# Six blocks of layer 2's modulation vectors move from TensorE products to VectorE, four of them into the scan stage

## The chip, the cores and the metric

The kernel runs on one core of one Trainium2 chip. The metric is the device time of one execution in microseconds. Before the change three runs gave 2504.61, 2489.74 and 2491.8 us, with a median of 2491.8 us.

## The reference

The reference is a two-layer trunk over 256 latent tokens and 256 context tokens, width 2048, batch 1. Each layer takes its shift, scale and gate from a conditioning vector, one for the latent tokens (`c`) and one for the context tokens (`c_ctx`).

```python
def adaln_params(cond, w_mod, b_mod):
    return jnp.split(jax.nn.silu(cond) @ w_mod + b_mod, 3, axis=-1)   # shift, scale, gate: 3 x 2048

def modulate(x, gain, shift, scale):
    return rmsnorm(x, gain) * (1 + scale) + shift

def na_mla_layer(x, ctx, c, c_ctx, ...):       # layer 1
    sh, sc, gt = adaln_params(c, w_mod, b_mod)
    hx = modulate(x, norm, sh[:, None], sc[:, None]) @ w_in     # the same for ctx with c_ctx
    ...                                        # 8 neighbourhood heads, 8 latent (MLA) heads
    y = (jnp.concatenate([merge_heads(o_na), merge_heads(o_mla)], axis=-1) * jax.nn.silu(z)) @ w_out
    x = x + gt[:, None] * y                    # ctx too
```

Layer 2 is a gated DeltaNet. Its input is `modulate(...) @ w_in` of both streams. After a short convolution, 32 value heads are scanned in chunks of 64 tokens in two directions, and the result goes through a gated output projection, `x + gt * y`. In layer 2 only the latent tokens are carried on, so its gate is needed for one of the two conditioning vectors, its shift and scale for both. A final RMSNorm ends the trunk.

## The kernel before

A modulation vector of one layer has 6144 columns, cut into 12 chunks of 512: chunks 0 to 3 are the shift, 4 to 7 the scale, 8 to 11 the gate. The weights of a chunk are 16 tiles of 128 x 512, 4 MB in all. The conditioning is `cond`, with one column for each of the two streams (samples, in the code). There are two ways of making a chunk:

- `adaln` (lines 122 to 159), the product on TensorE. Eight loads `mraw` of 512 KB bring the chunk; 16 matmuls `pmod<-mraw,cond` in four column strips of the array sum it up, VectorE copies the sum (`macc`), four transposes `pmt` bring it to one column per 128 values, and VectorE reduces it into `mod`.
- `adaln_lanes` (lines 161 to 192), on VectorE. For each of the 16 tiles and each sample one instruction on all 128 lanes, `lacc = mraw * cond + lacc` (the first of the 16 is a plain multiplication); at the end eight one-column matmuls `pml` against ones sum over the partitions, and VectorE adds the bias.

Both are generators, which a stage of the kernel advances a little at a time: `unit` (a 2048-row product for 128 output rows, in three passes `whi*hx`, `whi*hxlow`, `wlo*hx`, L90 to L92) advances the generator in `ahead` twice, and the loop over the latent heads once a head. A scheduler then sets each engine's order from the dependences and its own costs. Where a call names `after`, the instructions are held behind that matmul in the order of their engine.

The stages on the profile's clock, with what they make of the modulation vectors:

1. Layer 1's projections and its neighbourhood heads 0 to 6, to about 580 us. Layer 1's gate and layer 2's chunks 0 and 1 are made here on VectorE.
2. The latent ranks, 580 to 691 us: the last neighbourhood head's products, and `craw`, eight 512-wide products of 2048 rows, normalised into `cx`. No modulation work.
3. The latent heads (MLA), from 691 us to 900.9 us, where the last value product `po` ends. Here `ahead = later(mr, ((1, (2, 3, 8), 0),))` (L472) makes chunks 2, 3 and 8 by products, and L495 chunk 9, also by products.
4. The output projection with `gx` as its input, until 1066 us: 16 `unit`s. L512 starts `later(mr, ((1, (4, 5, 6, 7), 1),), last_mm)`, the scale chunks on VectorE.
5. The boundary to layer 2, 1066 to about 1145 us. L521 makes chunks 10 and 11 by products. `rstd_bcast` brings the norm's factor `rb`; `modulate` makes layer 2's input `hx` from it, with ScalarE (L236, L241), VectorE (L235, L238) and GpSimd (L243).
6. Layer 2's projections and its head preparation, to about 1742 us.
7. The scans, from about 1742 us. Here the order on TensorE, VectorE and ScalarE is the order of the code (`manual_schedule`). The loop goes over steps `st`; a step runs one chunk of 64 tokens for a pair of value heads in each of two chains (context, and six steps behind it the latent tokens), and, as filler on TensorE, 24 matmuls of the value projection. A step takes some 9.7 us. Weights are loaded as `raw`, three ahead, and split into `whi` (ScalarE) and `wlo` (VectorE). The chain of a step begins with `pks` (L1033); VectorE makes two `R` (L1037) of it, TensorE goes on with `ptr` (L1045), and at the end `ptr` (L1078) is added to `rf` on VectorE (L1083). Every second step ends with the convolution's taps (0, 4) on VectorE (L585), and every fourth has the output's `re` (L1111) behind them.
8. The output projection of layer 2, the gate, and the final norm.

Of the kernel before, what the change touches and what calls it, by code (L numbers as in the profile page):

```python
# [8 lines left out]
F32 = mybir.dt.float32  # L9
F32R = mybir.dt.float32r  # L10
AF = mybir.ActivationFunctionType
ALU = mybir.AluOpType
# [4 lines left out]
KT = 16  # L17
S = 256
T = 512
# [7 lines left out]
def trunk_kernel(ctx: ExitStack, tc: tile.TileContext, g):  # L27
# [16 lines left out]
    def cst(name, shape, src=None):  # L44
        t = const.tile(shape, F32, name=name, tag=name)
        if src is not None:
            nc.scalar.dma_start(t, src)
        return t
# [14 lines left out]
    ab_bmod, dn_bmod = vecs[:, 56:104], vecs[:, 104:152]  # L63
    o_gain = vecs[:, 152:153]
    mods = [cst(f"mod{l}", [128, 48, 2]) for l in range(2)]
    Am = [cst(f"Am{l}", [128, KT, 2]) for l in range(2)]


# [92 lines left out]
    def adaln_lanes(l, ps, pm, tp, chunks, after=None):  # L161

        wm, bmod, gain = ((g["ab_wm"], ab_bmod, ab_gain), (g["dn_wm"], dn_bmod, dn_gain))[l]
        for ch in chunks:
# [26 lines left out]
                V.tensor_tensor(Am[l][:, f], Am[l][:, f], gain[:, f].unsqueeze(2).broadcast_to([128, 4, 2]), op=ALU.mult)  # L191
            yield

    def steps(it, n=1000):
        for _ in range(n):
            if next(it, it) is it:
                break
# [62 lines left out]
    with tc.tile_pool(name="s0", bufs=2) as tp, tc.tile_pool(name="s0p", bufs=1, space=PSUM) as ps:  # L260
        V.memset(cond, 0.0)
        A.activation(cond[:, :, 0:2], cc, AF.Silu)
        xs = ((xA, g["xT"]), (xB, g["cT"]))
        for j in range(0, KT, 4):
            for x, src in xs:
# [53 lines left out]
    with tc.tile_pool(name="ab", bufs=2, reuse_waits="tile") as tp, \  # L319
# [105 lines left out]
        cr = tc.alloc_tile_pool(name="cr", bufs=1, reuse_waits="tile")  # L425


        craw = cr.tile([128, 8, T], F32, name="craw", tag="craw")
        rbl = []
        rbl2 = tp.tile([128, 2, T], F32, name="rbl", tag="vt", bufs=1)  # L430
# [13 lines left out]
        def roped(p, scale, parts_of):  # L444
            out = tp.tile([128, T], F32, name="rope", tag="rope", bufs=1)
            if scale == 1.0:
                A.copy(out, p)
            else:
                A.mul(out, p, scale)
            pp = ps.tile([128, S], F32, name="pp", tag="tr", bufs=TR)  # L450
            PE.matmul(pp, perm, out[:, :S], start=True, stop=True)
            t = tp.tile([128, S], F32, name="rtmp", tag="mtmp")
            V.tensor_tensor(t, pp, sinT, op=ALU.mult)
            V.tensor_tensor(out[:, :S], out[:, :S], cosT, op=ALU.mult)
            V.tensor_tensor(out[:, :S], out[:, :S], t, op=ALU.add)
            for r, hi, lo in parts_of:
                both(hi, lo, out[r])

        kr = tp.tile([128, 2, T], F32R, name="kr", tag="kr", bufs=1)
        roped(krp, 1.0, [(slice(0, 128), kr[:, 0], kr[:, 1])])  # L460
        na7 = na_head(7)
        cx = parts_tile("cx")
        ch, qr = cx[:, 0], cx[:, 1]
# [5 lines left out]
                V.tensor_tensor(ch[:, 8 + j], craw[:, j], ch[:, j].bitcast(F32), op=ALU.subtract)  # L469
        cr.release()  # L470
        mr = tc.alloc_tile_pool(name="mr2", bufs=2, reuse_waits="tile")
        ahead = later(mr, ((1, (2, 3, 8), 0),))  # L472

        rows = slice(0, 64), slice(64, 128)
        attend(*na7)
# [16 lines left out]
            attend(*o, 8 + h, None, ([qr[:, 2 * h + i] for i in range(2)], [kr[:, i] for i in range(2)]))  # L492

        steps(ahead)
        steps(later(mr, ((1, (9,), 0),), last_mm))  # L495
        pace = 0
        gx = parts_tile("gx")
        gh, gl = gx[:, 0], gx[:, 1]
# [19 lines left out]
            if j % 4 == 3:  # L518
                nc.sync.dma_start(x1d[:, j - 3:j + 1], x1[0][:, j - 3:j + 1])
        steps(ahead)  # L520
        ahead = later(mr, ((1, (10, 11), 0),), last_mm)  # L521
        rb = rstd_bcast(blocks_of(qacc, sq), 4, D, ps, "st", tp)
        hx = parts_tile("hx")
        hh, hl = hx[:, 0], hx[:, 1]
        modulate(1, lambda k, s: x1[s][:, k], rb, hh, hl, tp)
        steps(ahead)
        mr.release()

    abx.release()
# [110 lines left out]
    with tc.tile_pool(name="dn", bufs=2, reuse_waits="tile") as tp, \  # L640
# [288 lines left out]
        room = {}  # L929
# [192 lines left out]
        W += [g["dn_wo"][u][:, 1024 * c:1024 * c + 1024] for u, c in wo_order]  # L1122
        raws, wt = [], []

        def hi():
            j = len(wt)
            if j < len(W):
                while len(raws) < min(len(W), j + 3):
                    raws.append(load_raw(W[len(raws)]))
                h = wp.tile([128, 1024], F32R, name="whi", tag="whi", bufs=3)  # L1130
                A.copy(h, raws[j])  # L1131
                wt.append([h])
# [22 lines left out]
        def nothing():  # L1155
            return iter(())
# [59 lines left out]
        outs = early()  # L1216
        GATES = {56: (0, 4, 8), 57: (12, 16), 58: (20,), 66: (24,)}
        LAG = 6
        fins = nothing()
        for st in range(-2, 64 + LAG):  # L1220
            i, n = st // 4, st % 4
# [66 lines left out]
                take(fins, 1)  # L1288
            if vals and st % 2 == 1:
                prev = cur  # L1290
            for k in GATES.get(st, ()):
                gate(k, 4)
            if st == 68:
# [146 lines left out]
```

## Time and profile before

| | |
|---|---|
| runs | 2504.61, 2489.74, 2491.8 us, median 2491.8 |
| profiled execution | 2493.04 us, its span in the profile 2491.2 us |
| mean granted TensorE clock | 0.992 |
| TensorE matmuls | busy 2428.2 us (97%) |
| VectorE | busy 1762.8 us (71%) |
| ScalarE | busy 1105.6 us (44%) |
| GpSimd | busy 161.1 us (6%) |
| loads of layer 2's modulation weights | 96 of 512 KB |

An engine's share is an average over all eight stages; what an engine does in one of them is read from the windows of that stage. The chain that ended last is the path followed back from the last instruction, each step to what released it; a row of it says which line held the end of the kernel up and for how long. In a group of instructions, "idle before" is the time for which the engine stood idle just ahead of them, with what ended it. L numbers are lines of the kernel.

### The profile page before, as it was taken

What the parts mean: (1) busy time and instruction counts of PE and PEld (TensorE: products, weight loads), DVE (VectorE), ACT (ScalarE), POOL (GpSimd) and SP (SyncE); (2) the same over time, 40 slices, a digit from 0 to 9 for tenths busy, and PEclk for the clock granted to TensorE, in tenths of its full rate; (3) what the DMA queues carried; (4) which work ended last, traced back from release to release, by engine and by line L of the source; (5) the groups of instructions that cost most, each with busy time, mean ns of one, the idle gap of its engine ahead of it and who ended that gap; (6) DMA issues with size and microseconds to landing.
All of it is one profiled execution on the core that took longest, in us unless ns stands there. A gap on an engine that the chain in (4) does not pass through costs nothing.

```text
span 2491.2 us, 42483 instructions
## 1 busy us (share of the span) xinstructions
PE 2428.2 (97%) x16110; PEld 1963.1 (79%) x16110; DVE 1762.8 (71%) x3538; ACT 1105.6 (44%) x2446; POOL 161.1 (6%) x165
## 2 busy tenths in 40 slices
PE   6999999999989999999999999999999999999998
PEld 4557888888858878858998989987777777777787
DVE  4654678883356687856998988885777777777765
ACT  4223332333254432257565655634444544445453
POOL 0000000000000000020011101000000000012000
PEclk9999999999999999999999999999999999999999
DMA  8872645542253366664665666774343333336454
GB/s 252 282 277 87 200 154 172 169 157 84 88 187 110 102 198 204 226 210 136 195 173 158 179 178 180 204 201 108 87 116 103 115 112 98 106 100 184 148 193 141
DMA packets 254940, 397.24 MB, mean 159 GB/s; under 512 B 122257, under 2 KB 163857, under 8 KB 254609
## 3 DMA queue, kind: packets, MB, share of 16 engines
q1 hardware_dynamic: 253584, 393.00, 52.0%
q8 instruction: 127, 2.08, 0.3%
q10 hardware_dynamic: 1152, 1.54, 0.2%
q14 instruction: 77, 0.62, 0.1%
HBM read 356.94 MB, written 35.39 MB: 157 GB/s over the span
## 4 chain that ended last, share of the span: by engine, by line
PE 88%; issue 5%; DMA 3%; DVE 2%; ACT 1%; SPq 0%; POOL 0%; DVEq 0%; POOLq 0%; ACTq 0%
PE mm L90 21%; PE mm L91 20%; PE mm L92 20%; PE pks L1033 3%; PE pmod L141 3%; PE ptr L1045 2%; PE sp L365 2%; PE mm L105 2%; PE po L365 1%; DMA mraw<-dn_wm 1%; PE ptr L1078 1%; PE psu L1064 1%; PE pks L1064 1%; PE pt L398 1%; PE mm L107 1%
## 5 line engine op out<-in xcount | busy, mean ns | idle before, releaser
L90 PE MATMUL mm<-hx,whi 128*128 128x512 f32 (+1 forms) x2304 | 843.7, 366 | 2.3 <-ACT t L664 2.2
L91 PE MATMUL mm<-hx,whi 128*128 128x512 f32 (+1 forms) x2304 | 820.6, 356 | 2.5 <-issue 2.5
L92 PE MATMUL mm<-hx,wlo 128*128 128x512 f32 (+1 forms) x2304 | 819.4, 356 | 0.6 <-DVE wlo L78 0.6
L77 ACT CAST whi<-raw 128x1024 fp32r<-128x1024 f32 (+2 forms) x346 | 338.6, 980 | 701.4 <-PE mm L91 502.3
L78 DVE TENSOR_TENSOR wlo<-raw,whi 128x1024 fp32r<-128x1024 f32 (+2 forms) x346 | 394.3, 1142 | 204.3 <-ACT whi L77 198.2
L90 PEld LDWEIGHTS mm<-hx,whi 128*128 128x128 f32 x2304 | 438.8, 190 | 106.3 <-issue 27.0
L92 PEld LDWEIGHTS mm<-hx,wlo 128*128 128x128 f32 x2304 | 438.6, 190 | 65.1 <-issue 4.2
L91 PEld LDWEIGHTS mm<-hx,whi 128*128 128x128 f32 x2304 | 438.8, 190 | 61.4 <-issue 9.2
L177 DVE SCALAR_TENSOR_TENSOR lacc<-mraw,cond,lacc 128x512 f32<-128x512 f32 x300 | 208.6, 746 | 0.7 <-DMA mraw<-dn_wm 0.7
L585 DVE SCALAR_TENSOR_TENSOR acc<-cin,taps,acc 128x508 f32<-128x508 f32 (+3 forms) x256 | 187.2, 731 | 20.3 <-ACT acc L576 17.2
L105 PE MATMUL mm<-hx,whi 128*128 128x512 f32 x480 | 173.1, 404 | 0.1
L1055 DVE SCALAR_TENSOR_TENSOR vl<-ptr,egm,vh 128x128 fp32r<-128x128 f32 x224 | 64.7, 346 | 95.1 <-ACT rf L1052 37.9
L107 PE MATMUL mm<-hx,wlo 128*128 128x256 f32 x457 | 128.4, 281 | 1.3 <-DVE wlo L1139 1.2
L141 PE MATMUL pmod<-mraw,cond 128*32 128x512 f32 (+2 forms) x640 | 98.4, 508 | 28.1 <-DMA mraw<-ab_wm 18.8
L1139 DVE TENSOR_TENSOR wlo<-raw,whi 128x1024 fp32r<-128x1024 f32 x84 | 102.5, 1221 | 13.5 <-ACT whi L1131 13.4
L105 PEld LDWEIGHTS mm<-hx,whi 128*128 128x128 f32 x480 | 88.9, 188 | 24.5 <-issue 5.0
L816 DVE SCALAR_TENSOR_TENSOR outer<-L,bv,X 128x31 f32<-128x31 f32 (+15 forms) x248 | 99.4, 401 | 6.4 <-POOL X L811 0.5
L90 PE MATMUL mm<-gx,whi 128*128 128x512 f32 x256 | 100.3, 394 | 3.4 <-DVE x1B L515 2.4
L599 ACT ACTIVATE ac<-acc 128x128 f32<-128x128 f32 x160 | 37.4, 300 | 144.2 <-DVE acc L585 144.1
L91 PE MATMUL mm<-gx,whi 128*128 128x512 f32 x256 | 100.4, 392 | 0.5 <-DVE gx L503 0.5
L92 PE MATMUL mm<-gx,wlo 128*128 128x512 f32 x256 | 99.8, 391 | 0.0
L1049 ACT ACTIVATE vh<-ptr,egm 128x128 fp32r<-128x128 f32 x224 | 71.3, 374 | 57.1 <-PE ptr L1045 55.2
(301 smaller groups left out, 3648.5 us busy)
## 6 DMA issues: line engine op xcount, KB each, us to landing
raw<-dn_w SPq DMA_DIRECT2D x194, 512.0 KB
mraw<-dn_wm SPq DMA_DIRECT2D x96, 512.0 KB
mraw<-ab_wm SPq DMA_DIRECT2D x88, 512.0 KB
raw<-ab_w SPq DMA_DIRECT2D x66, 512.0 KB
raw<-dn_wo SPq DMA_DIRECT2D x64, 512.0 KB
raw<-ab_wo SPq DMA_DIRECT2D x32, 512.0 KB
raw<-ab_w SPq DMA_DIRECT2D x32, 256.0 KB
spt<-sp SPq DMA_DIRECT2D x64, 128.0 KB
```

Of the source, the lines that this page charges most:

```text
L77: A.copy(hi[:, :m], raw[:, :m])
L78: V.tensor_tensor(lo[:, :m], raw[:, :m], hi[:, :m].bitcast(F32), op=ALU.subtract)
L90: PE.matmul(ps, wh[:, c], xh[:, k0 + k, sl], start=first and k == 0, stop=False)
L91: PE.matmul(ps, wh[:, c], xl[:, k0 + k, sl], start=False, stop=False)
L92: end = PE.matmul(ps, wl[:, c], xh[:, k0 + k, sl], start=False, stop=last and k == kt - 1)
L105: PE.matmul(p2, wh[:, c], x[:, :, k0 + k], start=start, stop=stop)
L107: PE.matmul(p2[:, 0], wl[:, c], x[:, 0, k0 + k], start=False, stop=False)
L141: PE.matmul(pmod[32 * q:32 * q + 32, :m], cond[:, 4 * kg + q, :], raw[c // 1024][:, half + c % 1024:half + c % 1024 + m], start=kg == 0, s ...
L177: V.scalar_tensor_tensor(acc[:, s], raw[:, q], cond[:, k, s:s + 1], acc[:, s], op0=ALU.mult, op1=ALU.add)
L585: V.scalar_tensor_tensor(o3[:, :, i0:i1], p3[:, :, i0 + d:i1 + d], taps[:, ch, t:t + 1], o3[:, :, i0:i1], op0=ALU.mult, op1=ALU.add)
L816: V.scalar_tensor_tensor(o, L[:, rows, k:k + 1].broadcast_to([128, n, m]), bv[:, k:k + 1], X[:, k:k + 1, cols].broadcast_to([128, n, m]), ...
L1139: V.tensor_tensor(w, raws[j], h.bitcast(F32), op=ALU.subtract)
```

## The change

A new generator `lanes` makes a chunk on VectorE for `n` samples. Its loads come from the buffers of the weights (`raw`, four, shared with the products' weights), one load ahead.

```
+    cond1 = cst("cond1", [128, KT, 1])
...
+    def lanes(l, chunks, acc_of, cnd, n, pt_of):
+        wm, bmod = ((g["ab_wm"], ab_bmod), (g["dn_wm"], dn_bmod))[l]
+        tiles = [(ch, t) for ch in chunks for t in range(8)]
+        load = lambda ch, t: load_raw(wm[ch, t // 2][:, t % 2 * 1024:t % 2 * 1024 + 1024])
+        ahead = load(*tiles[0])
+        yield
+        for i, (ch, t) in enumerate(tiles):
+            raw, ahead = ahead, load(*tiles[i + 1]) if i + 1 < len(tiles) else None
+            if t == 0:
+                acc = acc_of(ch)
+            for q in range(2):
+                k = 2 * t + q
+                for e in range(n):
+                    x = raw[:, 512 * q:512 * q + 512]
+                    if k == 0:
+                        V.tensor_scalar(acc[e], x, cnd[:, k, e:e + 1], None, op0=ALU.mult)
+                    else:
+                        V.scalar_tensor_tensor(acc[e], x, cnd[:, k, e:e + 1], acc[e], op0=ALU.mult, op1=ALU.add)
+            yield
+            if t == 7:
+                pt = pt_of(n)
+                for j in range(4):
+                    for e in range(n):
+                        PE.matmul(pt[:, j, e:e + 1], acc[e][:, j * 128:j * 128 + 128], ones[:, 0:1], start=True, stop=True)
+                f = slice(4 * ch, 4 * ch + 4)
+                V.tensor_tensor(mods[l][:, f, :n], pt, bmod[:, f].unsqueeze(2).broadcast_to([128, 4, n]), op=ALU.add)
...
+        A.copy(cond1, cond[:, :, 0:1])
...
+        ahead = lanes(1, (2, 3), lambda ch: [tp.tile([128, T], F32, name="lacc", tag="bias") for _ in range(2)], cond, 2,
+                      lambda n: ps.tile([128, 4, n], F32, name="pml", tag="pm", bufs=1))
         craw = cr.tile([128, 8, T], F32, name="craw", tag="craw")
...
+        steps(ahead)
         na7 = na_head(7)
...
-        ahead = later(mr, ((1, (2, 3, 8), 0),))
+        ahead = iter(())
...
-        steps(later(mr, ((1, (9,), 0),), last_mm))
         pace = 0
...
-        ahead = later(mr, ((1, (10, 11), 0),), last_mm)
         rb = rstd_bcast(blocks_of(qacc, sq), 4, D, ps, "st", tp)
...
         modulate(1, lambda k, s: x1[s][:, k], rb, hh, hl, tp)
-        steps(ahead)
...
+        depth = 3
         def hi():
...
-                while len(raws) < min(len(W), j + 3):
+                while len(raws) < min(len(W), j + depth):
...
+        gates = lanes(1, range(8, 12), lambda ch: [room["e"][:, 3072 + 512 * (ch % 2):3584 + 512 * (ch % 2)]], cond1, 1,
+                      lambda n: ps.tile([128, 4, n], F32, name="pml", tag="tr", bufs=1))
...
+            if st == 3:
+                depth = 2
+            if 4 <= st < 56:
+                depth = 2 if next(gates, 0) is None else 3
```

So chunks 2 and 3 (shift) are made for both samples between the `craw` products, the gate's chunks 8 to 11 for the latent sample alone at the end of 32 scan steps, one load and two instructions a step, summed up in free columns of a scan tile (`re`). While they run, the scans' weights are loaded two ahead and not three.

The calls for the scale chunks are not touched in the code, but the scheduler's order changes around them. The first place is VectorE at the start of the latent heads, just behind the last `cx`. Before, the softmax of the last neighbourhood head follows at once (`mx`, `rc`, `pr`), with `vt`, `PT` (copies from PSUM) and a weight's `wlo`:

```order
L469 TENSOR_TENSOR cx<-craw,cx 128x512 x5
L358 TENSOR_TENSOR vt<-pv,vt 128x512
L394 RECIPROCAL rc<-sm 128x1
L395 TENSOR_SCALAR pr<-pr,rc 128x512
L389 TENSOR_REDUCE mx<-sp 128x1
L394 RECIPROCAL rc<-sm 128x1
L395 TENSOR_SCALAR pr<-pr,rc 128x512
L78 TENSOR_TENSOR wlo<-raw,whi 128x512
L358 TENSOR_TENSOR PT<-pt,PT 128x4x128
```

Now, with line numbers moved by the new code (by 1 to 34 here):

```order
L503 TENSOR_TENSOR cx<-craw,cx 128x512 x5
L176 TENSOR_SCALAR lacc<-mraw,cond 128x512 x2
L389 TENSOR_TENSOR vt<-pv,vt 128x512
L178 SCALAR_TENSOR_TENSOR lacc<-mraw,cond,lacc 128x512 x2
L425 RECIPROCAL rc<-sm 128x1
L178 SCALAR_TENSOR_TENSOR lacc<-mraw,cond,lacc 128x512 x2
L426 TENSOR_SCALAR pr<-pr,rc 128x512
L420 TENSOR_REDUCE mx<-sp 128x1
L425 RECIPROCAL rc<-sm 128x1
L178 SCALAR_TENSOR_TENSOR lacc<-mraw,cond,lacc 128x512 x2
L420 TENSOR_REDUCE mx<-sp 128x1
L79 TENSOR_TENSOR wlo<-raw,whi 128x512
```

The `lacc` rows are the scale chunks 4 to 7. They stood in the output projection before, and now stand between the softmax instructions of the latent heads: all 128 of them come ahead of the split of `gx`. Their loads moved with them on the load queue, to between the latent heads' weights, where the loads of the products stood.

The second place is VectorE at the end of a scan step with `st % 4 == 0`. Before, the taps and `re` are followed by the next step's `R`:

```order
L1083 TENSOR_TENSOR rf<-rf,ptr 128x256
L585 SCALAR_TENSOR_TENSOR acc<-cin,taps,acc 128x2x254 x2
L1111 SCALAR_TENSOR_TENSOR re<-pot,ngain,re 128x512
L1037 SCALAR_TENSOR_TENSOR R<-pks,neg,ra 128x128 x2
L1037 SCALAR_TENSOR_TENSOR R<-pks,neg,vc 128x128 x2
```

Now (the same lines are L1114, L616, L1142 and L1068):

```order
L1114 TENSOR_TENSOR rf<-rf,ptr 128x256
L616 SCALAR_TENSOR_TENSOR acc<-cin,taps,acc 128x2x254 x2
L1142 SCALAR_TENSOR_TENSOR re<-pot,ngain,re 128x512
L214 SCALAR_TENSOR_TENSOR re<-raw,cond_85,re 128x512 x2
L1068 SCALAR_TENSOR_TENSOR R<-pks,neg,ra 128x128 x2
L1068 SCALAR_TENSOR_TENSOR R<-pks,neg,vc 128x128 x2
```

The gate's two instructions of a step (`cond_85` is `cond1`) stand behind everything of the step and ahead of the next step's `R`; at the other steps with gate work they stand in the same place, behind `rf` alone or behind `rf` and the taps.

The third place is TensorE at the boundary to layer 2. Before, the products of chunks 10 and 11 stand between the norm's sums, `rb` and layer 2's first products:

```order
L204 MATMUL ss<-ones,sq 128x1
L141 MATMUL pmod<-mraw,cond 32x512 x6
L213 MATMUL rb<-dg,ones 128x128 x4
L141 MATMUL pmod<-mraw,cond 32x512 x2
L90 MATMUL mm<-hx,whi 128x512 x2
L141 MATMUL pmod<-mraw,cond 32x512 x4
L91 MATMUL mm<-hx,whi 128x512
```

Now:

```order
L234 MATMUL ss<-ones,qacc 128x1
L234 MATMUL ss<-ones,sq 128x1
L243 MATMUL rb<-dg,ones 128x128 x4
L91 MATMUL mm<-hx,whi 128x512 x2
L92 MATMUL mm<-hx,whi 128x512
L93 MATMUL mm<-hx,wlo 128x512
```

Nothing is left between them, there and in the rest of the boundary. In the latent heads no `pmod` and no `pmt` is left either; 65 of the output projection's matmuls stand ahead of the last `po` there, where 90 did before.

## The prediction

> **What bounds the kernel now.** I read the page's engine shares and the chain that ended last, then the windows of each stage that the change touches, then the groups and single rows behind them.
>
> ```profile
> PE 2428.2 (97%) x16110; PEld 1963.1 (79%) x16110; DVE 1762.8 (71%) x3538; ACT 1105.6 (44%) x2446; POOL 161.1 (6%) x165
> PE 88%; issue 5%; DMA 3%; DVE 2%; ACT 1%; SPq 0%; POOL 0%; DVEq 0%; POOLq 0%; ACTq 0%
> ```
>
> Over the whole span TensorE is the bound, with 88% of the chain, and VectorE has 29% of the span free. Read no further, and every product moved to VectorE looks like a gain. The stages say otherwise. The columns are the window, its length, busy time of PE, PEld, DVE, ACT and POOL with instruction counts, granted clock, DMA share and GB/s.
>
> ```profile
> 540.00:560.00 20.00, 20.00 (x97) 16.58 (x96) 19.92 (x33) 6.64 (x12) 0.00 (x0) 1.00 0.56 177
> 580.00:690.90 110.90, 110.40 (x512) 91.55 (x510) 38.69 (x52) 30.93 (x40) 2.02 (x2) 1.00 0.27 86
> 690.90:900.90 210.00, 203.07 (x1076) 151.05 (x1076) 133.07 (x291) 99.23 (x217) 0.00 (x0) 0.99 0.43 139
> 907.00:1066.00 159.00, 159.00 (x723) 132.45 (x723) 125.72 (x190) 37.44 (x56) 0.00 (x0) 0.99 0.68 218
> 1066.00:1112.00 46.00, 42.97 (x201) 24.48 (x202) 28.29 (x58) 26.59 (x61) 17.36 (x14) 0.93 0.65 208
> 1742.00:2239.00 497.00, 497.00 (x3086) 385.27 (x3085) 364.33 (x954) 238.39 (x736) 36.82 (x39) 1.00 0.36 105
> ```
>
> The last neighbourhood head (540 to 560) has both engines full. The latent ranks (580 to 690.9) leave VectorE 72 us free. The latent heads (690.9 to 900.9) leave it 77 us. The output projection and the scans are full on TensorE and nowhere else. Only at the boundary (1066 to 1112) does TensorE itself stand.
>
> The prices of a chunk both ways, in the page's group of multiply-adds and the groups between 690 and 1115 us:
>
> ```profile
> L177 DVE SCALAR_TENSOR_TENSOR lacc<-mraw,cond,lacc 128x512 f32<-128x512 f32 x300 | 208.6, 746 | 0.7 <-DMA mraw<-dn_wm 0.7
> L141 PE MATMUL pmod<-mraw,cond 128*32 128x512 f32 x192 | 44.2, 644 | 9.1 <-DMA mraw<-dn_wm 9.1
> L150 PE MATMUL pmt<-ident,macc 128*128 128x128 f32 x24 | 3.9, 277 | 0.8 <-DVE macc L147 0.8
> L184 PE MATMUL pml<-ones,lacc 128*128 128x1 f32 x64 | 7.4, 246 | 0.0
> ```
>
> VectorE: 208.6 us over 300 is 0.695 us; in a run of five it is 0.68 (3.40 us, a row below). So 32 instructions for two samples are 22 us, 16 for one are 11 us. TensorE: six chunks take 48.1 us, 9.9 us of waits beside them, 9.7 us a chunk. The one-column sums `pml` cost 7.4/4 = 1.9 us a chunk for two samples, about 1 us for one.
>
> **The change part by part.** The sum goes against the profiled execution, 2493.0 us (span 2491.2), which is 1.2 us above the median of the three runs.
>
> *Chunks 2 and 3 beside the latent ranks: +8 us.* That is 64 instructions, 64 x 0.68 = 44 us on VectorE, against 72 us free. But the order puts chunk 2 into the softmax of neighbourhood head 6, where VectorE is busy 19.92 of 20 us: it has no room there, though TensorE has ranks to go on with. Two `pml` sums are 3.9 us on TensorE. For the rest I bound what a late `wlo` costs: nothing, if the ranks cover it all, up to 12 us, about half of chunk 2's 22, if they don't. Since in the ranks' window TensorE waited only 0.5 us and VectorE 72, I take the near end, 4 us. Together +8, range +4 to +16.
>
> *Chunks 2, 3, 8 and 9 out of the latent heads, the scale chunks into them: +2 us.* This is the step on which the forecast turns. The chain here is held by the products:
>
> ```profile
> 696.48 3.98 DMA mraw<-dn_wm
> 711.97 3.84 DMA mraw<-dn_wm
> 718.67 4.14 DMA mraw<-dn_wm
> 723.95 4.47 DMA mraw<-dn_wm
> 895.99 8.21 DMA mraw<-dn_wm
> ```
>
> Some 16 us of waits for weights at the start of the stage go, and two thirds of the 44.2 us of `pmod`. TensorE's busy time of 203.1 would come down by four sixths of the 48.1 us, to some 171 us in a stage of 210. But the scheduler uses the room at once: all 128 instructions of chunks 4 to 7 stand ahead of the `gx` split. On VectorE the stage then has 133.1 us as before, less 7.7 for the eleven `lacc` that were there already and 2.8 for four `macc`:
>
> ```profile
> L177 DVE SCALAR_TENSOR_TENSOR lacc<-mraw,cond,lacc 128x512 f32<-128x512 f32 x11 | 7.7, 748 | 0.0
> L147 DVE COPY macc<-pmod 128x512 f32<-128x512 f32 x4 | 2.8, 692 | 1.7 <-PE pmod L141 1.6
> 896.54 3.40 DVE L177 SCALAR_TENSOR_TENSOR lacc<-mraw,cond,lacc 128x512 f32<-128x512 f32 x5
> ```
>
> plus 128 x 0.68 = 87.0 us. That is 209.6 us of work in a stage that took 210.0. VectorE takes its instructions in order, the first `lacc` stands ahead of the last neighbourhood head's softmax, and its load can start no earlier than that of the first product did, which cost 3.98 us. So the last `po` comes at 209.6 plus about 2 to 4 us of waits, where it came at 210.0: TensorE's 32 us of saved work there buy nothing, as the bound changes hands. I take +2. Below: some split work for the later stage (`gx`, `wlo`) lies in the 133 and can go behind the last `po`, 12 us at most, −10. Above: VectorE loses a tenth of the stage's 210 to waits for softmax steps between, as it idled for such steps before, +12 after what is already in the sum.
>
> A rule of the Trainium skill bears on the price. The Trainium skill's page "VectorE: DVE Perf Modes" (Mode 1× (REGULAR) — the baseline) has this kind of instruction give one result a cycle; with the 0.96 GHz that the page states, 512 results would be an estimated 0.53 us, the 128 would take 68 us, and the stage would end some 17 us earlier. By that page the sum would be 17 us lower; the rows' 0.68 decides against it.
>
> *The output projection: −4 us.* Of its 768 large matmuls (16 units of 48) the order has 90 ahead of the last `po` before and 65 now. So it had 678 to do behind 900.9, with `pml` and the end of chunk 9 between, and was done at 1066, in 165 us. The window from 907 gives the pitch: 159.0 us, less 64 `pml` at 0.12, over 659 matmuls is 0.23 us. Now it is 703 with nothing between: 703 x 0.23 = 161 us. Bounds −6 to 0.
>
> *The boundary: −7 us.* Two waits of VectorE for chunks 10 and 11, with ScalarE's groups between 1074 and 1115 us:
>
> ```profile
> 1087.69 0.69 DVE L147 COPY macc<-pmod 128x512 f32<-128x512 f32 x1 [3.85 <-PE pmod L141]
> 1112.70 0.69 DVE L147 COPY macc<-pmod 128x512 f32<-128x512 f32 x1 [8.43 <-PE pmod L141]
> L236 ACT ACTIVATE hx<-mh,mod 128x256 fp32r<-128x256 f32 x32 | 14.7, 497 | 14.0 <-DVE mh L235 14.0
> L241 ACT ACTIVATE mh<-mh,mod 128x256 f32<-128x256 f32 x22 | 10.5, 494 | 0.0
> ```
>
> `modulate` behind `rb` took 1074 to about 1105 us; ScalarE's own work in it is 25.2 us, and the 8.43 us behind it were waited for chunk 11's products alone. All 12.3 us cannot go, since TensorE has 96 large matmuls of layer 2 to do there (22 us at 0.23) that trail the last `hx`. I take −7, between −3 (the first wait alone) and −12 (both).
>
> *The gate in the scans: +17 us.* Each of 32 steps gets one load and two dependent multiply-adds, 1.45 us by the distance of the taps' pair (1869.28 to 1870.72). TensorE is full here, its order is fixed, and `R` stands behind the pair. So the price is whatever of 1.45 us the room between `R` and its `ptr` does not take:
>
> ```profile
> 1868.94 0.42 DVE L1083 TENSOR_TENSOR rf<-rf,ptr 128x256 f32<-128x256 f32 x1 [0.22 <-PE ptr L1078]
> 1869.28 1.53 DVE L585 SCALAR_TENSOR_TENSOR acc<-cin,taps,acc 128x508 f32<-128x508 f32 x2
> 1870.72 0.60 DVE L1037 SCALAR_TENSOR_TENSOR R<-pks,neg,ra 128x128 f32<-128x128 f32 x2
> 1871.24 0.60 DVE L1037 SCALAR_TENSOR_TENSOR R<-pks,neg,vc 128x128 f32<-128x128 f32 x2
> 1872.46 0.60 PE L1045 MATMUL ptr<-R,re 128*128 128x128 f32 x4
> 1880.01 0.61 DVE L1037 SCALAR_TENSOR_TENSOR R<-pks,neg,ra 128x128 f32<-128x128 f32 x2 [0.60 <-PE pks L1033]
> 1882.08 0.61 PE L1045 MATMUL ptr<-R,re 128*128 128x128 f32 x4
> 1888.61 0.42 DVE L1083 TENSOR_TENSOR rf<-rf,ptr 128x256 f32<-128x256 f32 x1 [1.14 <-PE ptr L1078]
> 1890.39 0.75 DVE L1111 SCALAR_TENSOR_TENSOR re<-pot,ngain,re 128x512 f32<-128x512 f32 x1
> 1891.05 0.60 DVE L1037 SCALAR_TENSOR_TENSOR R<-pks,neg,ra 128x128 f32<-128x128 f32 x2
> 1891.57 0.60 DVE L1037 SCALAR_TENSOR_TENSOR R<-pks,neg,vc 128x128 f32<-128x128 f32 x2
> 1892.12 0.60 PE L1045 MATMUL ptr<-R,re 128*128 128x128 f32 x4
> ```
>
> Odd steps, 16 of the 32, have no taps at their end. At 1880 VectorE had idled 0.60 us and `R` was done 1.46 us ahead of `ptr`: 2.06 us of room, so nothing. Steps ending in taps (1868.94): `R` is done at about 1871.76 where its first is asked for at 1872.46, by its first half 1.14 us earlier; 1.45 less about 0.95 leaves 0.5 us, 8 times, 4 us. Steps ending in taps and `re` (1888.61): the last `R` is done at 1892.17 with `ptr` at 1892.12, and the first at 1891.65, 0.47 us of room; less the 0.18 that the halves overlap, 1.16 us are left, 8 times, 9 us. Four `pml` at about 1 us are 4 us more. Together +17. At the low end only the sums and half the rest, +8; at the high end, steps of both kinds at the whole 1.45 and some of the odd ones, +30. The loads ahead fall from three to two while DMA is 36% busy; I cost that at nothing, and if weights came late, a step's `wlo` would show it.
>
> Sum: 8 + 2 − 4 − 7 + 17 = +16, so 2509 against the profiled execution and **2508 us** against the median.
>
> **The rivals.**
>
> (a) *TensorE's savings count in full.* With 48 + 10 us of products and waits gone and only the `pml` sums added (3.9 + 4), the time is 2492 − 50 = 2442. For it: 88% of the chain. Against it: 209.6 us of VectorE work in the latent heads, and the order at the steps' ends.
>
> (b) *The scans hide the pairs.* Only `pml` is left there: 2508 − 13 = 2495, no change. For it: VectorE is busy 364 of 497 us in the scans. Against it: the room at 1892.
>
> (c) *Slower: every pair is on the path.* The mechanism is the place of the pair, between `rf` and `R` in the chain that crosses VectorE and TensorE each step; if TensorE's filler cannot be drawn ahead, as its order is fixed, 32 x 1.45 = 46 us stand in place of 13, 2508 + 33 = 2541. It decides as soon as the odd steps' 2 us of room are spent, for instance when a step that was delayed brings `pks` later to the next. For it: TensorE never idles in 497 us, so no delay is made up. Against it: the idle 0.60 at 1880.
>
> (d) *The clock.* Around the waits of 3.98 and 3.84 us the granted clock fell:
>
> ```profile
> 700.00:720.00 20.00, 18.82 (x86) 8.92 (x86) 8.55 (x22) 7.37 (x17) 0.00 (x0) 0.91 0.64 216
> 740.00:760.00 20.00, 20.00 (x112) 15.42 (x111) 12.47 (x26) 9.28 (x20) 0.00 (x0) 1.00 0.49 148
> ```
>
> If TensorE, waiting for VectorE, ran all of the latent heads at 0.91, its 171 us of work would take 17 us more; at worst all of it lies on the path between softmax steps, 2525. Against it: single waits must be that long, and some 40 us of idle time over 32 softmaxes would rather come in small pieces. The Trainium skill's page "TensorE: Matmul & The Clock Gate" (Part 1: The HAM clock gate) states a drop to half rate after an idle window of about 3.4 us; by that rule this rival needs gaps of that length, and the trace's 0.91 beside waits of 4 us agrees.
>
> **How the numbers follow.** Within 1%, 2466.9 to 2516.7 us, is about what a measurement of this kernel can't tell from no change. The forecast has 0.50, its own range 2490 to 2525 by the bounds above, a fifth of it above 2516.7; (a) 0.05, (b) 0.20, (c) 0.20, (d) 0.05. Faster: (a) and a trace of the rest, 0.06. Slower: 0.10 of the forecast, (c), and most of (d), 0.33. Within 1%: 0.61. The range goes from 2482, which holds (b) with its bounds, to 2545, which takes in (c); (a) is left out with what lies beyond (c).
>
> **What the changed profile would show.** Latent heads: VectorE over 95% busy, TensorE's share down to some 80%, the last `po` at about 212 us behind the start of the stage; if VectorE has idle time and `po` ends 20 us earlier, the second step is wrong. Ranks: `wlo` before PE waits of a few us. Boundary: no wait on `pmod`, `modulate` in under 30 us. Scans: the steps with `re` at their end longer by 1.2 us, the odd ones as before, and the first step behind chunk 11 again as before; all 32 longer alike is (c), none is (b). If the clock in the latent heads is below 0.95, (d) is at work. What would make all of it wrong is a stage that the change should leave alone: layer 2's projections and head preparation, 597 us long, are partly reordered as well.

## The result, and the profile after

| | before | changed |
|---|---|---|
| median of the runs | 2494.07 us (4 runs: the three above and 2496.34) | 2525.28 us (2523.56 to 2526.51, 4 runs) |
| ratio | | 1.0123, 95% interval 1.01 to 1.0145 |
| span of the profiled execution | 2491.2 us | 2524.7 us |
| mean granted TensorE clock | 0.992 | 0.984 |

The kernel became slower by 1.2%, 33.5 us between the profiled spans, where 0.65%, 16 us, was forecast: the sign was right, and the forecast was half of the change. In the page's shares and the engines of the chain that ended last, VectorE has gone from 2% to 11% of the chain, and TensorE from 88% to 75%:

```profile
PE 2421.9 (96%) x15958; PEld 1978.1 (78%) x15958; DVE 1838.0 (73%) x3654; ACT 1107.0 (44%) x2447; POOL 158.5 (6%) x165
PE 75%; DVE 11%; issue 6%; DMA 3%; ACT 3%; SPq 1%; POOL 0%; DVEq 0%; POOLq 0%; ACTq 0%
```

To see where, I took one landmark for each end of a stage from the views of single tiles. A row gives the durations' minimum, median and maximum and the starts of the first and the last of these instructions. Before:

```profile
L434 ACT COPY craw<-mm x8: 581/583/591, 571.7 to 641.8; 128x512 f32<-128x512 f32 x8
L469 DVE TENSOR_TENSOR cx<-craw,cx x8: 679/682/683, 690.9 to 695.7; 128x512 fp32r<-128x512 f32 x8
L405 DVE TENSOR_TENSOR goB<-po,goB x16: 416/425/426, 328.0 to 900.9; 128x256 f32<-128x256 f32 x16
L515 DVE SCALAR_TENSOR_TENSOR x1A<-mm,mod,xr x16: 476/484/485, 905.6 to 1066.0; 128x256 f32<-128x256 f32 x16
L1033 PE MATMUL pks<-St,kq x192: 379/379/430, 1704.6 to 2304.4; 128*64 128x256 f32 x192
L1078 PE MATMUL ptr<-rh,rc x128: 270/275/341, 1761.8 to 2365.3; 128*128 128x128 f32 x128
```

The changed kernel:

```profile
L467 ACT COPY craw<-mm x8: 577/585/592, 579.7 to 658.3; 128x512 f32<-128x512 f32 x8
L503 DVE TENSOR_TENSOR cx<-craw,cx x8: 679/682/684, 709.1 to 713.9; 128x512 fp32r<-128x512 f32 x8
L436 DVE TENSOR_TENSOR goB<-po,goB x16: 403/414/425, 329.9 to 926.6; 128x256 f32<-128x256 f32 x16
L548 DVE SCALAR_TENSOR_TENSOR x1A<-mm,mod,xr x16: 473/484/485, 932.9 to 1086.6; 128x256 f32<-128x256 f32 x16
L1064 PE MATMUL pks<-St,kq x192: 378/379/430, 1720.7 to 2337.6; 128*64 128x256 f32 x192
L1109 PE MATMUL ptr<-rh,rc x128: 270/275/297, 1778.7 to 2398.3; 128*128 128x128 f32 x128
```

The differences of neighbouring landmarks are the stages' lengths:

| stage, between landmarks | before | changed | difference | forecast |
|---|---|---|---|---|
| start to the first `craw` | 571.7 | 579.7 | +8.0 | |
| first to last `craw` (the ranks) | 70.1 | 78.6 | +8.5 | +8 for these three |
| last `craw` to the first `cx` | 49.1 | 50.8 | +1.7 | |
| first `cx` to the last `goB` (latent heads) | 210.0 | 217.5 | +7.5 | +2 |
| to the last `x1A` (output projection) | 165.1 | 160.0 | −5.1 | −4 |
| to the first `pks` (boundary, layer 2's heads) | 638.6 | 634.1 | −4.5 | −7 |
| to the last `ptr` (scans) | 660.7 | 677.6 | +16.9 | +17 |
| to the end | 125.9 | 126.4 | +0.5 | |

Of the seventeen microseconds beyond the forecast, 10 are in the first three rows and 5.5 in the latent heads. The other three steps came within 3 us of their terms.

**The ranks.** The first row's 8.0 us are lost ahead of the products, in neighbourhood head 6. Chunk 2's multiply-adds stand there between head 6's softmax and the work that VectorE already had, and VectorE is full (its 36.84 us are the third busy time in the row):

```profile
542.00:580.00 38.00, 34.62 (x169) 29.03 (x168) 36.84 (x63) 10.74 (x20) 0.00 (x0) 0.96 0.50 159
```

From 532 us to the first `craw` at 579.7 the chain of the changed kernel runs through VectorE for 35 of its 48 us, with one wait for a load (4.05 us at 542.04); before the change the same stretch of the chain is TensorE alone. Behind the first `craw` the chain is TensorE's, with one break (start, duration, what):

```profile
624.24 1.47 PE pml L220 x14
625.74 0.49 DVE lacc L212
...
627.27 0.76 DVE lacc L214
628.04 3.69 DMA raw<-ab_w
631.81 1.05 ACT whi L78
632.88 1.24 DVE wlo L79
634.17 0.50 PE mm L93
```

TensorE stands 3 us for this weight (2.5 for its `whi`, 0.5 for its `wlo`, until 634.17), and its next matmuls come 0.43 us apart where they are 0.23 elsewhere; so did the first ones behind head 6. With 1.5 us for the sums these make up the 8.5. The load queue's timeline shows why it came late:

```profile
606.17 0.33 SPq L72 DMA_DIRECT2D raw<-ab_w  x1
612.38 0.33 SPq L72 DMA_DIRECT2D raw<-dn_wm  x1
628.04 0.33 SPq L72 DMA_DIRECT2D raw<-ab_w  x1
```

For 22 us no weight of the products (`ab_w`) is asked for. Two of the four `raw` buffers hold the first tiles of chunk 3; chunk 3's first instruction (L212) waits for chunk 2's sums `pml`, which want the PSUM buffer in which the norm's `rb` stood until 619 us:

```profile
619.05 0.69 DVE L470 COPY rbl<-rb 128x512 f32<-128x512 f32 x1 [4.63 <-PE rb L243]
625.74 0.49 DVE L212 TENSOR_SCALAR lacc<-raw,cond 128x512 f32<-128x512 f32 x1 [3.22 <-PE pml L220]
```

**The latent heads.** The windows of the stage, as a whole and its start and rest (length, busy time of PE, PEld, DVE, ACT, POOL, granted clock, DMA share, GB/s):

```profile
709.10:926.60 217.50, 186.57 (x972) 154.16 (x973) 196.35 (x405) 98.49 (x216) 0.00 (x0) 0.95 0.39 121
709.10:760.00 50.90, 29.87 (x120) 23.22 (x121) 44.34 (x86) 22.89 (x38) 0.00 (x0) 0.80 0.47 150
760.00:926.60 166.60, 156.69 (x854) 130.94 (x853) 152.01 (x320) 75.60 (x178) 0.00 (x0) 0.99 0.36 113
```

VectorE is busy 90% of the stage, TensorE 86%. The first 51 us hold most of TensorE's loss: 21 us of idle time there, and a clock of 0.80. Before the change the chain ran through TensorE for some 181 us of this stage and through VectorE for 9; now it runs through VectorE for some 123 us (53 of them `lacc`) and through TensorE for 64, with 15 us of waits for loads. It begins with the wait for the first load, as forecast:

```profile
714.63 3.87 DMA mraw<-dn_wm
718.60 0.88 DVE lacc L176 x2
```

### The profile page after: what moved, and what is told of

The parts are those of the page before. It is cut to its first block, busy times and chain, and to the rows that moved or that the text cites. A ratio compares the mean times of both kernels' runs of the same rounds, so it can differ in the third digit from the quotient of the medians.

```text
span 2524.7 us, 42320 instructions
## 1 busy us (share of the span) xinstructions
PE 2421.9 (96%) x15958; PEld 1978.1 (78%) x15958; DVE 1838.0 (73%) x3654; ACT 1107.0 (44%) x2447; POOL 158.5 (6%) x165
## 4 chain that ended last, share of the span: by engine, by line
PE 75%; DVE 11%; issue 6%; DMA 3%; ACT 3%; SPq 1%; POOL 0%; DVEq 0%; POOLq 0%; ACTq 0%
PE mm L91 18%; PE mm L92 17%; PE mm L93 17%; PE pks L1064 3%; DVE lacc L178 3%; PE ptr L1076 2%; PE mm L106 2%; PE pmod L142 2%; DVE wlo L79 2%; DVE acc L616 1%; PE ptr L1109 1%; PE sp L396 1%; PE psu L1095 1%; PE po L396 1%; PE mm L108 1%
## 5 line engine op out<-in xcount | busy, mean ns | idle before, releaser
L616 DVE SCALAR_TENSOR_TENSOR acc<-cin,taps,acc 128x508 f32<-128x508 f32 (+3 forms) x256 | 183.1, 718 | 17.7 <-ACT acc L607 14.4
L340 DVE TENSOR_TENSOR zs<-zs,mm 128x512 f32<-128x512 f32 x72 | 49.1, 686 | 67.7 <-PE mm L93 67.5
```

What stands on the lines that cost most here:

```text
L616: V.scalar_tensor_tensor(o3[:, :, i0:i1], p3[:, :, i0 + d:i1 + d], taps[:, ch, t:t + 1], o3[:, :, i0:i1], op0=ALU.mult, op1=ALU.add)
```

## The experiments

All are the changed kernel with one edit or with several, timed against the kernel before on the same chip.

**1. No shift chunks in the ranks.** The generator is left out.

```
-        ahead = lanes(1, (2, 3), ...)
+        ahead = iter(())
```

> The changed kernel without chunks 2 and 3 (the shift columns 1024 to 2047 of layer 2 are zero), all else as changed. Theory: these 64 VectorE instructions and their loads cost what the traces show between the end of neighbourhood head 5 and the last cx, some 16 us, so about 2509 us (2525 - 16), and the last craw copy is again some 70 us behind the first. Rival: the stretch is late for another reason (the scheduler's other order there), then 2520 or more.

Measured: 2504.06 us, ratio 1.004 (1.0026 to 1.0053), 21 us under the changed kernel. The first `craw` is at 572.6 and the eight products take 70.1 us, to the tenth as before the change:

```profile
L467 ACT COPY craw<-mm x8: 578/582/593, 572.6 to 642.7; 128x512 f32<-128x512 f32 x8
```

So the shift chunks made this stretch longer: 17.3 of the 18.2 us to the first `cx` are gone. The other few microseconds lie between the last `x1A` and the first `pks` (627 us where the changed kernel has 634), a stretch that the edit doesn't touch; it varies from 626 to 634 between these kernels, and why stays open.

**2. No gate in the scans.** `gates` is empty and the weights are loaded three ahead throughout.

```
-        gates = lanes(1, range(8, 12), ...)
+        gates = iter(())
```

> The changed kernel without the gate chunks 8 to 11 in the scans (the gate of layer 2 is zero), weights three ahead throughout. Theory: the scans' 17 us go, about 2508 us, and the stage from the first pks to the last ptr takes 661 us as before the change, not 678. Rival: the scans are longer because of the shifted start of their loads or the reordered preparation, then 2518 or more.

Measured: 2505.08 us, ratio 1.0044 (1.0029 to 1.0058). The scans take 660.5 us, as before. The gate's work costs 17 us there; this edit takes away the pairs, their loads, their sums and the shallower loading of the weights all at once, and experiment 4 tells the pairs' place from the rest.

**3. The scale chunks held to the output projection.** `adaln_lanes` takes as its conditioning a copy that depends on the last latent head.

```
+        held = tp.tile([128, KT, 2], F32, name="held", tag="held", bufs=1)
+        for s in range(2):
+            V.scalar_tensor_tensor(held[:, :, s], go[1][:, KT - 1, 0:KT], 0.0, cond[:, :, s], op0=ALU.mult, op1=ALU.add)
```

> The changed kernel with the scale chunks' conditioning copied through an instruction that reads the last latent head's output, so that their 128 VectorE instructions stand in the output projection, as before the change. Theory: VectorE bound the latent heads; with some 171 us of work TensorE sets the stage, 180 to 190 us and not 217, the output projection stays at 160 us, and the whole is 2490 to 2500 us. Rival: the stage is held by its start (first loads, rotary steps, half clock) whatever VectorE has to do, then 2518 to 2525.

Measured: 2492.53 us, ratio 0.9997 (0.9986 to 1.0008): the whole loss is gone by this edit alone. The windows of the latent heads and the output projection in this kernel:

```profile
705.70:891.10 185.40, 170.75 (x908) 144.11 (x909) 119.96 (x264) 96.95 (x216) 0.00 (x0) 0.97 0.19 60
891.10:1057.10 166.00, 165.06 (x754) 137.30 (x753) 140.24 (x216) 41.50 (x62) 0.00 (x0) 1.00 0.67 219
```

The heads take 185.4 us, with TensorE's work at the forecast's 171, and the output projection hides the 128 instructions at 6 us more than without them. The rival, a stage held by its start, is out: without the products the stage would be 24.6 us shorter than before the change, and it was 7.5 us longer because the scheduler drew the scale chunks into the room that they left. The edit moves the chunks' loads together with their instructions; waits for loads are 15 us of the changed kernel's chain here, so VectorE's work has the larger part of the 32.1 us, and the two were not separated. In the two stages together the edit gains 26 us (32.1 less 6.0). The profiled span is 36.2 us shorter; of the other 10 us, 3.4 stand ahead of the stage and 7.9 in the uneven stretch of experiment 1, with the scans 1.5 longer, and these weren't traced further.

**4. The gate's pair behind `R`.** The same two instructions a step, called behind the step's two `R` instead of ahead of them.

```
             take(X, 1)
             take(C, 1)
+            if 5 <= st < 56:
+                depth = 2 if next(gates, 0) is None else 3
             hi()
...
-            if 4 <= st < 56:
-                depth = 2 if next(gates, 0) is None else 3
```

> The changed kernel with the gate's two instructions a step called behind the step's two R and not ahead of them. Theory: the pair costs only where it delays R, so the scans fall from 678 to about 665 us (the sums stay), 2512 us. Rival: VectorE's 1.45 us a step are on the chain wherever they stand, then 2522 to 2528.

Measured: 2510.81 us, ratio 1.0063 (1.0045 to 1.0081). The scans take 666.8 us, 10.8 less than the changed kernel's. The pair's place in the changed kernel's VectorE timeline, at a step ending in taps, and in this one:

```profile
1890.96 1.52 DVE L616 SCALAR_TENSOR_TENSOR acc<-cin,taps,acc 128x508 f32<-128x508 f32 x2
1892.40 1.53 DVE L214 SCALAR_TENSOR_TENSOR re<-raw,cond,re 128x512 f32<-128x512 f32 x2
1893.85 0.60 DVE L1068 SCALAR_TENSOR_TENSOR R<-pks,neg,ra 128x128 f32<-128x128 f32 x2
```

```profile
1882.44 1.52 DVE L616 SCALAR_TENSOR_TENSOR acc<-cin,taps,acc 128x508 f32<-128x508 f32 x2
1883.88 0.60 DVE L1068 SCALAR_TENSOR_TENSOR R<-pks,neg,ra 128x128 f32<-128x128 f32 x2
1884.40 0.60 DVE L1068 SCALAR_TENSOR_TENSOR R<-pks,neg,vc 128x128 f32<-128x128 f32 x2
1884.92 1.53 DVE L214 SCALAR_TENSOR_TENSOR re<-raw,cond,re 128x512 f32<-128x512 f32 x2
```

The pair costs where it delays `R` and little behind it. The length of each step is the distance of its `rf` row from the next step's. Here is a step that ends in taps and `re`, before (9.69 us) and in the changed kernel (10.69 us):

```profile
1888.61 0.42 DVE L1083 TENSOR_TENSOR rf<-rf,ptr 128x256 f32<-128x256 f32 x1 [1.14 <-PE ptr L1078]
1898.30 0.42 DVE L1083 TENSOR_TENSOR rf<-rf,ptr 128x256 f32<-128x256 f32 x1 [1.07 <-PE ptr L1078]
1911.11 0.42 DVE L1114 TENSOR_TENSOR rf<-rf,ptr 128x256 f32<-128x256 f32 x1 [1.15 <-PE ptr L1109]
1921.80 0.42 DVE L1114 TENSOR_TENSOR rf<-rf,ptr 128x256 f32<-128x256 f32 x1 [1.08 <-PE ptr L1109]
```

Over the 32 steps with gate work:

| steps ending in | count | longer by, each | together | forecast |
|---|---|---|---|---|
| taps | 8 | 0.82 | 6.6 | 4 |
| taps and `re` | 8 | 0.98 to 1.00 (the first 0.31) | 7.2 | 9 |
| neither | 16 | 0.0, but 0.8 in the four behind a chunk's end, which hold its sums | 3.2 | 4 |

With the pair behind `R` the first two kinds are as before the change. Of the 6 us that are left over the kernel before, the sums make 3.6 (four steps, 0.9 each), four other steps 0.3 each, and 1.3 come later.

**5. The shift chunks started behind head 6.** Their conditioning depends on that head's output, as in 3.

> The changed kernel with the shift chunks' conditioning copied through an instruction that reads neighbourhood head 6's output, so that chunk 2 starts behind that head's softmax. Theory: the first 6 us of the loss (first craw copy at 578 us and not 572) come from chunk 2's instructions in a stretch where VectorE has no room; they go, the later 8 stay, 2517 to 2520 us. Rival: chunk 2 is only late by its own loads; then the first craw copy stays at 578, or the ranks behind it lengthen by as much, 2524 to 2528.

Measured: 2527.17 us, ratio 1.0141 (1.0123 to 1.0159). The theory held in its first half and fell in its second: the first `craw` is 9.5 us earlier, but the ranks lose 10.2.

```profile
L470 ACT COPY craw<-mm x8: 576/584/588, 570.2 to 659.0; 128x512 f32<-128x512 f32 x8
```

The eight products take 88.8 us. In this kernel's chain a second wait for a weight has come up beside the one at 629, at the start of chunk 2 (`575.92 3.51 DMA raw<-ab_w`). So the 8 us ahead of the first `craw` come from starting chunk 2 inside head 6, as the chain there shows; but started later it costs the ranks as much, by waits for weights.

**6. Chunk 2 alone.**

```
-        ahead = lanes(1, (2, 3), ...)
+        ahead = lanes(1, (2,), ...)
```

> The changed kernel with chunk 2 alone made beside the ranks (the shift columns 1536 to 2047 of layer 2 are zero). Theory: the later 8 us come from chunk 3's first instruction, which waits for chunk 2's sums behind the norm's rb, while the weight buffers that its loads fill are held; without chunk 3 the eight craw products take 70 us as before the change and not 78, and the time is about 2515. Rival: it is the work of chunk 2 itself, then 75 us or more and 2520.

Measured: 2518.62 us, ratio 1.0106 (1.009 to 1.0122); the first `craw` at 578.8, the eight products 72.6 us:

```profile
L468 ACT COPY craw<-mm x8: 580/584/592, 578.8 to 651.4; 128x512 f32<-128x512 f32 x8
```

Of the 8.5 us in the ranks 6 go with chunk 3, 2.5 stay (1.7 of them are chunk 2's sums), and so do 7.1 of the 8.0 us ahead of the first `craw`. The total is 3.6 us above the theory's number.

**7. Loads of their own.** The shift chunks' loads go into two buffers in the space of `PT`, free between head 6 and the last head, on the same queue.

```
+        slots = tp.tile([128, 2, 1024], F32, name="slots", tag="PT", bufs=1)
...
+            def load(ch, t):
+                nc.sync.dma_start(slots[:, t % 2], wm[ch, t // 2][:, t % 2 * 1024:t % 2 * 1024 + 1024])
+                return slots[:, t % 2]
```

> The changed kernel with the shift chunks' loads in two buffers of their own (the space of the attention's PT, free from the end of neighbourhood head 6), no longer in the weights' four; the loads stay on the same queue as the weights. Holding chunk 2 back only moved the loss from head 6 into the ranks, so the theory now is that the loads keep weights waiting. If by holding the buffers: first craw copy at 571, the eight craw products in 72 us, 2510 to 2513 us. Rival: by standing ahead of the weights in the one load queue; then the products take 80 us or more and the time is 2520 or more.

Measured: 2506.41 us, ratio 1.0058 (1.0041 to 1.0075), 19 us under the changed kernel and 2 us above having no shift chunks at all.

```profile
L472 ACT COPY craw<-mm x8: 573/579/588, 572.3 to 644.2; 128x512 f32<-128x512 f32 x8
572.30:695.10 122.80, 122.33 (x582) 102.06 (x581) 82.93 (x122) 35.02 (x46) 2.02 (x2) 1.00 0.47 152
```

The same 64 VectorE instructions now cost the ranks the two sums' time and nothing more; TensorE is busy 122.3 of 122.8 us. The space of `PT` also holds chunk 2 back to the end of head 6, as in experiment 5, so the two are to be compared with each other: with the same late start and the same queue, the ranks take 88.8 us with shared buffers and 71.9 with buffers of their own. Behind the first `craw`, then, what cost was the sharing of the four weight buffers, not VectorE's time and not the queue's order. The 8 us ahead of it are another matter: they go with the late start, here as in experiment 5, and were VectorE's time in head 6.

**8. The same with GpSimd issuing the loads.** `nc.gpsimd.dma_start` in place of `nc.sync.dma_start`.

> The same with these loads issued by GpSimd and not on the weights' queue. Both theories have 2510 to 2513 us here; if it stays above 2518, neither buffers nor queue, but VectorE's work itself (44 us beside the weights' splits) or the transfers are what makes the ranks longer.

Measured: 2511.91 us, ratio 1.0084 (1.0069 to 1.0099). Both theories' number, but not for their reason: the first `craw` comes at 570.4, the products take 78.6 us. Its chain has a wait that the other queue has not, and VectorE's timeline shows what it held up:

```profile
600.56 7.30 DMA slots<-dn_wm
607.96 1.41 DVE L218 SCALAR_TENSOR_TENSOR lacc<-slots,cond,lacc 128x512 f32<-128x512 f32 x2 [2.11 <-DMA slots<-dn_wm]
611.75 0.15 DVE L240 TENSOR_SCALAR ms<-ss 128x4 f32<-128x4 f32 x1
612.67 1.05 POOL rs L242
```

The norm's sums `ss` are done at 601.4, but VectorE takes them up (`ms`) only at 611.75, behind multiply-adds that waited 1.7 and 2.1 us for these loads; `rs` follows at once on GpSimd, and TensorE stands 3.8 us ahead of `rb`. A new wait took the place of the old one.

**9 to 12. Combinations.** The two edits that helped most:

> The changed kernel with both edits that helped: the scale chunks held to the output projection and the gate's pair behind R. Theory: the gains lie in different stages and add, 2525 - 33 - 14 = 2478 us, 0.6% under the kernel before. Rival: they overlap (a chain that the one shortens is bounded by the other), 2485 or more.

Measured: 2480.4 us, ratio 0.9954 (0.9939 to 0.9969). They add: 45 us of the expected 47. With chunk 2 started late and the sums in another PSUM buffer besides:

> The same with the shift chunks started behind head 6's softmax and their sums in a PSUM buffer that the rank's norm doesn't use, so that chunk 3 need not wait for rb. Theory: 6 us for the first and about 3 to 6 for the second, 2466 to 2470 us. Rival: neither, 2478.

Measured: 2482.47 us, ratio 0.9965 (0.9949 to 0.998), no gain in time: the first `craw` is at 570.5, 8.0 us earlier than with the two edits alone, and the products take 84.5 us, 6.4 more; the uneven stretch of experiment 1 is 4 us longer. Against the 88.8 us of experiment 5 the other PSUM buffer takes off 4.3, and the second wait for a weight is gone from the chain; the first, at 576.22, is left so long as the weight buffers are shared. With buffers of their own and GpSimd's queue:

> All that helped in one: scale chunks held to the output projection, the gate's pair behind R, the shift chunks' loads in their own buffers and issued by GpSimd. Theory: 2480 - 13 = 2467 us, about 1% under the kernel before. Rival: the later stages give some of it back, as when the shift chunks were started late, 2478 or more.

Measured: 2473.85 us, ratio 0.9935 (0.9921 to 0.9948), the rival's side of the middle; the ranks take 78.2 us as in experiment 8. And with the weights' queue:

> The three edits that helped: scale chunks held to the output projection, the gate's pair behind R, the shift chunks' loads in their own buffers on the weights' queue (GpSimd's queue was slower). Theory: the gains lie in three stages and add, 2525 - 33 - 14 - 18 = 2460 us, some 1.2% under the kernel before. Rival: as in the last combination some of it is given back in the preparation of layer 2's heads, 2470 or more.

Measured: 2467.37 us, ratio 0.9896 (0.988 to 0.9911). This beats both kernels: 1.0% under the one before, 58 us under the changed one. The gains stand in three stages: 71.9 us for the eight products, 186.3 for the latent heads, 666.0 for the scans; the theory's 2460 had counted 18 us for the loads' own buffers, which gave 13 over the kernel with the other two edits.

## Why the prediction was right or wrong

The forecast was too low by 17 us. The step that failed is the term for chunks 2 and 3 beside the ranks, 10 us of it; the term for the latent heads was short by another 5.5.

*Chunks 2 and 3 beside the ranks: +8 forecast, +18.2 measured*, 17.3 of it the chunks' own by experiment 1. The two sums were about right (3.9 forecast, 1.5 and 1.7 in the chain). The step that failed is "for the rest I bound what a late `wlo` costs", where I took 4 us of at most 12 and the runs show 15. The reason that I gave, 0.5 us of TensorE's waits and 72 us of VectorE's free time, is that of the ranks' window, and the loss has two parts that the window doesn't show. Some 8 us were lost ahead of it, in head 6, where I had written that VectorE has no room and yet counted on TensorE to cover it; experiments 5 and 7 have the first `craw` back at 570 to 572 with chunk 2 started behind that head. The other 7 us are 3 us of waiting for one weight and, behind this wait and behind head 6, matmuls at half clock. The `wlo` was late for a reason that I had not in mind: its weight had not been loaded, since chunk 3's loads held two of the four weight buffers through a wait of their own. Experiment 6 shows that part go with chunk 3, and experiments 5 and 7, set side by side, that the shared buffers make such a loss. The sharing was in the diff.

*The latent heads: the mechanism right, the size off, and nearer than its parts.* +2 was forecast, +7.5 measured. VectorE did become the bound, and the products' removal bought nothing; experiment 3 shows what it would have bought, 24.6 us. My sum had 209.6 us of VectorE work and 2 to 4 of waits; the profile has 196.4 us of work and 21 us without work. The price of the `lacc` was right (88.5 us for the 128, 87.0 forecast). The rest of the work takes 107.9 us beside them, where I had 122.6; a part of that is that instructions without a gap between them overlap by their ends, a `lacc` being 0.74 us long alone and starting 0.66 behind the one before. The waits that the trace lists come to 20 us: the first load, and many short ones of at most 3.2. The two largest:

```profile
DVE lacc L176 <- DMA mraw<-dn_wm: 4.0, 1, 4.0
DVE wlo L79 <- ACT whi L78: 4.0, 4, 1.7
```

So the waits were short by some 17 us and the work too long by 13, and it is luck that the two nearly cancel. I had named a tenth of the stage for the waits as the upper bound, and that is what they came to. TensorE's busy time is 186.6 us and not 171: 7.6 of the difference are the scale chunks' sums, which moved along and which I had not counted, and part of the rest is matmuls at half clock. The signs that I had named, VectorE over 95% busy and TensorE at 80%, came out as 90% and 86%.

The lower price of 0.53 us for a `lacc`, by which the stage would have ended earlier, did not come about. It counted results alone, and the rows have more than that: `mh`, with half the elements of a `lacc`, takes 0.47 us, which is more than half of 0.74. Besides, 128 times the difference to 0.68 is 19 us and not 17.

*The output projection* (−4, measured −5.1) held. At *the boundary* (−7, measured −4.5 to the first `pks`) the waits on `pmod` are gone, and the last `modulate` instruction of ScalarE comes 34 us behind the last `x1A` and not 39. The −4.5 itself says less than it seems: the same stretch is up to 8 us shorter in kernels whose edits leave it alone. TensorE, with nothing to do between the norm's sums and `hx`, has a lower clock over the 46 us behind the last `x1A`, 0.78 where it had 0.93.

*The scans* (+17, measured +16.9 and, by experiment 2, 17.1) held, and not by number alone: the steps that were to be longer are (experiment 4), the odd ones are not, and the sums take 3.2 us of the 4 forecast. Steps ending in taps cost more than I had (0.82 and not 0.5), those with `re` less (0.98 to 1.00 and not 1.16); that these two errors cancel is luck, of 2 us. The weights loaded two ahead, which I had put at nothing, cost at most the 2.5 us that experiment 4 leaves beside the sums.

*The rivals.* (a), TensorE's savings in full, is what experiment 3 and the last combination bring out in part; in the kernel as changed it was out. (b) was refuted by 2, (c) by the odd steps, which but for the sums are as long as before. (d) has a part, at the start of the latent heads, where the clock was 0.80 while VectorE worked off the softmax and the first chunk; over the stage it was 0.95, just at the bound that I had named. How much of the 7.5 us it makes was not separated.

## What to carry to other kernels

Before a change takes buffers or an engine's free time from a stage, list who else draws on them, and look at the stage where the order puts the work: here chunk 2 began in a head where VectorE was full, chunk 3's loads held half of the weights' buffers, and a scheduler filled the time that the products had left with work from a later stage. Work that is to stay in its stage needs a dependence that keeps it there; naming an instruction of another engine did not. In a chain that two engines share, the place of an instruction counts more than its time: here the 32 pairs cost some 14 us ahead of `R` and 1 to 3 behind it, the sums aside.

## What was not expected of the hardware

TensorE's clock was at half not only while TensorE stood idle but for the first 6 us of full work behind it. At the start of the latent heads TensorE has next to nothing to do from 738.4 to 745.0 us; the matmuls from 745 to 751 us come 0.43 apart where they are 0.23 elsewhere, and only then is the granted clock full again:

```profile
738.40:745.00 6.60, 0.02 (x1) 0.03 (x1) 6.54 (x13) 1.83 (x3) 0.00 (x0) 0.50 0.40 139
745.00:751.00 6.00, 6.00 (x14) 4.80 (x15) 5.10 (x10) 1.33 (x3) 0.00 (x0) 0.51 0.48 152
751.00:754.00 3.00, 3.00 (x23) 2.78 (x22) 1.40 (x3) 1.54 (x2) 0.00 (x0) 1.00 0.12 48
```

The Trainium skill's page "TensorE: Matmul & The Clock Gate" (Part 1: The HAM clock gate) has two states, half and full rate; the 0.50 here and the 1.00 of the full stages agree.

And a 512 KB load issued by GpSimd stood 6.4 to 7.3 us in the chain (experiment 8), where single loads on the other queue mostly stood 3.5 to 4.5 us. What part of it is the issue and what the transfer was not tried.
